# Seven low parts of the second layer's weights: from an adding DMA to a subtraction on VectorE

## The chip, the cores and the metric

The kernel runs on one core of one Trainium2 chip. The metric is the device time of one execution in microseconds (us), the median of several. TensorE is PE in the profile (PEld is its loading of weights), VectorE is DVE, ScalarE is ACT, GpSimd is POOL, SyncE is SP; a "q" behind an engine's name is its queue of DMA instructions.

## The reference, cut to what matters

Two layers over 256 latent tokens and 256 context tokens of 1024 channels. In the second layer (the last) the context gives keys and values only, so nearly all of its products run over 256 columns.

```python
for l in range(DEPTH):
    h = modulate(rmsnorm(x, norm1_g[l]), sh1, sc1)
    p = h @ w_in[l]                      # GLU, q, k, v, branch gates
    y_conv = conv_branch(p[..., :GLU_END], ...)   # depthwise conv of 31 taps, layernorm, silu, w_conv_out
    y_attn = merge_heads(neighbourhood_attention(q, k, v, k_c, v_c, rpb)) @ w_na_out[l]
    x = x + g1 * gated_merge(p[..., QKV_END:], y_conv, y_attn, w_out[l])
    h2 = modulate(rmsnorm(x, norm2_g[l]), sh2, sc2)
    x = x + g2 * conv_ffn(h2, w_up[l], ffn_dw[l], ffn_dw_b[l], w_down[l])
```

All of it is float32.

## The kernel before

Activations lie with their channels on the 128 partitions. The weights come in units of 128 x 1024 float32 (512 KB), each loaded by one DMA of SP into a tile `raw`. TensorE multiplies a narrower form of float32, so every operand is split into a high part and a low part (what the high part leaves), and each product is three matmuls (`mm3`): high weight by high input (L187), high weight by low input (L188), low weight by high input (L189). `group` does this for the eight 128 x 128 blocks of a unit, 24 matmuls into one PSUM bank; PSUM has four banks of the kind `main`.

The high part `whi` of a unit is a cast on ScalarE (L168 or L206). The low part `wlo` is made in one of two ways, and the table `ADDED` of (layer, unit) says which:

```python
    def wadded(l, u):
        r = raw_unit(wall[l, u])
        ...
        act.copy(hi, r)                             # L206
        act.mul(lo, hi.bitcast(F32), -1.0)          # L207
        pool.dma_start(lo, r, accum_op=ALU.add)     # L208
    def unit8(l, u, at=None):
        w = wadded(l, u) if (l, u) in ADDED else wunit(l, u, at)
```

In `wadded` ScalarE writes the negative of the high part and a DMA issued by GpSimd adds `raw` to it in SBUF. In `wunit` VectorE subtracts the high part from `raw` (L169, in `wparts`). `raw`, `whi` and `wlo` have four buffers each, so a unit's cast can begin when the unit four before it is used up.

The order of the work on each engine is set by the tile framework's scheduler, which weighs its own estimates of when each instruction can start; so a different way of making a low part also moves the instructions around it. Each engine then works its list off in order. SP's list of loads is in order too.

The second layer runs in this order: GLU and values; in turn a gate tile, a query tile and a key tile (`gate(ea, 0)`, `qk(1)`, `gate(ea, 1)`, `qk(2)`, `gate(ea, 2)`, `qk(3)`), with the softmax of earlier head pairs (L501 on VectorE, L504 and L507 on ScalarE) and the taps of the depthwise convolution (L659, VectorE) mixed in; the other gate tiles; the layer norm of the convolution's result; the two branch products; their gated sum (`z`, tiles `h`: L982 and L983 on VectorE, L984 on ScalarE, L985 on VectorE); eight units of the output projection (`U_WO`) with the residual (L990); the second norm; 22 pairs of units of the up-projection (`U_UP`: the i-th pair has unit i and unit 22+i, with the convolution of width 3 in L1053 on ScalarE and L1054 and L1057 on VectorE, then L1066, L1069, L1079, L1080); the down-projection.

Of the input projection (`U_IN`), unit 6+j holds the queries of head pair j, unit 10+j its keys, unit 14+n gate tile n.

Of the kernel before, what the change touches and what calls it, by code (L numbers as in the profile page):

```python
# [43 lines left out]

U_GLU0, U_V, U_IN, U_NA, U_CO, U_WO, U_UP, U_DN = 0, 2, 6, 36, 40, 44, 52, 96
NU = 118
ADDED = {*((0, U_IN + i) for i in (*range(19), 20, 22, 24, 26, 28)), *((0, u) for u in (U_NA + 1, U_NA + 3, *range(U_CO, U_CO + 4))), *((1, U_IN + i) for i in (7, 8, 9, 14, 15, 16)), (1, U_WO), *((1, U_UP + i) for i in (4, 5, 6))}
T_GLU, T_Q, T_K, T_GATE = 0, 6, 10, 14

SWAP16 = [(i + 16) % 32 for i in range(32)]  # L50
# [3 lines left out]
def trunk(ctx: ExitStack, tc: tile.TileContext, xt, cvec, crow, wall, wada, params, bias_t, rope_t, out):  # L54
# [123 lines left out]
    def wunit(l, u, at=None, cuts=1):  # L178
        w, more = wparts(l, u, at, cuts)
        more()  # L180
        return w

    def cols(w, i):
        return sl(w[0], i), sl(w[1], i)
# [16 lines left out]
    def wadded(l, u):  # L201

        r = raw_unit(wall[l, u])
        hi = wp.tile([P, UW], F32R, tag="whi", bufs=4, name=nm("whi"))
        lo = wp.tile([P, UW], F32R, tag="wlo", bufs=4, name=nm("wlo"))
# [3 lines that stand above are left out]
        return hi, lo  # L209

    def unit8(l, u, at=None):
        w = wadded(l, u) if (l, u) in ADDED else wunit(l, u, at)
        return [cols(w, i) for i in range(KD)]
# [404 lines left out]
    for l in range(DEPTH):  # L618
# [5 lines left out]
        with ExitStack() if last else start as e1a:  # L624
# [285 lines left out]
            with ExitStack() as e1c:  # L910
# [57 lines left out]
                def branch(base, xh, xl):  # L968
                    for n in range(0, KD, 2):
                        w = (wadded if (l, base + n // 2) in ADDED else wunit)(l, base + n // 2)  # L970
                        for i in range(2):
# [354 lines left out]
```

## Time and profile before

| what | before |
|---|---|
| median of 3 runs | 1116.0 us (1113.12 to 1118.12) |
| profiled execution | 1116.28 us, of which the span from first to last instruction is 1114.5 us |
| mean granted TensorE clock | 0.996 |
| busy share of the span: PE, PEld, DVE, ACT, POOL | 98%, 85%, 80%, 52%, 4% |
| adding transfers (`wlo<-raw`) | 40 of 512 KB, median 5.7 us from issue to landing |
| of these in the second layer | 10, issued from 762.34 to 946.62 us |

The second layer begins near 735 us of the span. A row of the timeline has the start in us, the duration in us, the engine, the line, the operation with output and inputs, and in brackets how long the engine was idle before it and what ended that. The end of a matmul is modelled, so how fast TensorE goes is read from the starts of successive matmuls.

### The profile page before, as it was taken

How to read it: one execution, taken by the hardware profiler on the slowest of the kernel's cores; microseconds unless marked ns; L12 is line 12 of the kernel's file. 1: busy time of each engine (PE TensorE's matmuls, PEld its weight loads, DVE VectorE, ACT ScalarE, POOL GpSimd, SP SyncE). 2: the span in 40 equal slices, each digit the busy share in tenths (PEclk: the TensorE clock that was granted, in tenths of full speed). 3: DMA queues.
4: the chain of work that ended last, by engine and by line, in shares of the span. 5: the costliest groups of instructions: out<-in, count | busy, mean ns of one | idle time of the engine just before them, and what ended most of it. 6: DMA issues, size and time to landing. Idle time of an engine off the chain costs nothing.

```text
span 1114.5 us, 18085 instructions
## 1 busy us (share of the span) xinstructions
PE 1096.1 (98%) x6896; PEld 952.3 (85%) x6896; DVE 887.7 (80%) x1623; ACT 575.9 (52%) x950; POOL 49.2 (4%) x66
## 2 busy tenths in 40 slices
PE   9999999999999999999999999999999999999997
PEld 7777777788889888888888888989799998999997
DVE  5568998889988888888887456797898886888773
ACT  4458766444334543434343223545875667666642
POOL 1011110011000000000000000001000000000000
PEclk9999999999999999999999999999999999999999
DMA  9988674988833454545467566548844584766681
GB/s 369 289 214 228 136 170 108 285 245 220 256 114 114 133 169 142 179 133 165 157 210 237 175 193 210 184 146 234 222 146 150 149 286 136 226 188 186 209 269 57
DMA packets 61238, 212.93 MB, mean 191 GB/s; under 512 B 7392, under 2 KB 7648, under 8 KB 61152
## 3 DMA queue, kind: packets, MB, share of 16 engines
q1 hardware_dynamic: 55104, 190.77, 52.9%
q0 software_dynamic: 5760, 20.97, 9.9%
q8 instruction: 54, 0.88, 0.3%
q14 instruction: 32, 0.26, 0.1%
q10 hardware_dynamic: 288, 0.04, 0.0%
HBM read 187.63 MB, written 1.05 MB: 169 GB/s over the span
## 4 chain that ended last, share of the span: by engine, by line
PE 89%; ACT 3%; DMA 3%; DVE 2%; issue 2%; SPq 1%; POOL 0%; DVEq 0%; ACTq 0%; POOLq 0%
PE main L187 26%; PE main L189 26%; PE main L188 26%; PE main L723 4%; DMA wlo<-raw 2%; SPq L715 1%; PE sc L187 1%; PE sc L188 1%; PE sc L189 1%; PE po L220 1%; PE po L563 1%; DVE cb L659 1%; ACT whi L206 1%; PE sc L137 1%; ACT wlo L207 1%
## 5 line engine op out<-in xcount | busy, mean ns | idle before, releaser
L189 PE MATMUL main<-h,wlo 128*128 128x256 f32 (+1 forms) x1328 | 444.8, 336 | 8.4 <-DMA wlo<-raw 8.4
L187 PE MATMUL main<-h,whi 128*128 128x256 f32 (+1 forms) x1328 | 447.8, 338 | 0.0
L188 PE MATMUL main<-h,whi 128*128 128x256 f32 (+1 forms) x1328 | 443.1, 334 | 0.1
L168 ACT CAST whi<-raw 128x1024 fp32r<-128x1024 f32 (+1 forms) x204 | 211.1, 1038 | 255.8 <-PE main L188 122.3
L169 DVE TENSOR_TENSOR wlo<-raw,whi 128x1024 fp32r<-128x1024 f32 (+1 forms) x204 | 245.2, 1207 | 99.6 <-ACT whi L168 91.9
L189 PEld LDWEIGHTS main<-h,wlo 128*128 128x128 f32 x1328 | 250.4, 189 | 37.8 <-DMA wlo<-raw 9.4
L187 PEld LDWEIGHTS main<-h,whi 128*128 128x128 f32 x1328 | 250.4, 189 | 30.3 <-issue 1.9
L188 PEld LDWEIGHTS main<-h,whi 128*128 128x128 f32 x1328 | 250.6, 189 | 28.5 <-DVE h L390 0.5
L659 DVE SCALAR_TENSOR_TENSOR cb<-u,par,cb 128x512 f32<-128x512 f32 (+1 forms) x240 | 144.6, 620 | 2.8
L188 PE MATMUL main<-fl,whi 128*128 128x256 f32 (+1 forms) x386 | 123.1, 319 | 0.0
L189 PE MATMUL main<-fh,wlo 128*128 128x256 f32 (+1 forms) x386 | 122.9, 318 | 0.0
L187 PE MATMUL main<-fh,whi 128*128 128x256 f32 (+1 forms) x386 | 122.8, 319 | 0.0
L293 DVE CUSTOM_DVE_ANT_0 t<-raw,sb,par 128x1024 bf16<-128x1024 f32 x72 | 91.6, 1280 | 0.8 <-DMA raw<-in_wada 0.5
L188 PEld LDWEIGHTS main<-fl,whi 128*128 128x128 f32 x386 | 72.7, 188 | 5.7 <-DVE fl L1080 0.2
L189 PEld LDWEIGHTS main<-fh,wlo 128*128 128x128 f32 x386 | 72.7, 188 | 5.6
L187 PEld LDWEIGHTS main<-fh,whi 128*128 128x128 f32 x386 | 72.6, 188 | 5.6
L206 ACT CAST whi<-raw 128x1024 fp32r<-128x1024 f32 x40 | 42.1, 1052 | 56.5 <-PE main L188 47.3
L1053 ACT ACTIVATE t<-main,par 128x512 f32<-128x512 f32 (+1 forms) x82 | 51.0, 670 | 36.8 <-PE main L189 36.7
L293 DVE CUSTOM_DVE_ANT_0 t<-own,sb,par 128x1024 bf16<-128x1024 f32 x48 | 60.5, 1282 | 2.0 <-DMA own<-in_wada 2.0
L1054 DVE SCALAR_TENSOR_TENSOR t<-main,par,t 128x510 f32<-128x510 f32 (+1 forms) x82 | 47.3, 615 | 10.8 <-ACT t L1053 10.7
L208 POOL DMA_DIRECT2D wlo<-raw x40 | 35.1, 878 | 314.9 <-ACT wlo L207 185.2
L1057 DVE SCALAR_TENSOR_TENSOR t<-main,par,t 128x510 f32<-128x510 f32 (+1 forms) x82 | 46.9, 612 | 0.0
(215 smaller groups left out, 1267.2 us busy)
## 6 DMA issues: line engine op xcount, KB each, us to landing
raw<-in_wall SPq DMA_DIRECT2D x239, 512.0 KB, 4.3
raw<-in_wada SPq DMA_DIRECT2D x64, 512.0 KB, 4.5
wlo<-raw POOLq DMA_DIRECT2D x40, 512.0 KB, 5.7
own<-in_wada SPq DMA_DIRECT2D x24, 512.0 KB, 5.7
bias<-in_bias_t SPq DMA_DIRECT2D x8, 520.0 KB, 5.5
row<-in_wada SPq DMA_DIRECT2D x8, 512.0 KB, 4.9
sb<-in_crow SPq DMA_DIRECT2D x5, 512.0 KB, 4.9
x<-in_xt SPq DMA_DIRECT2D x8, 256.0 KB, 3.9
```

What stands on the lines that cost most here:

```text
L168: act.copy(hi[:, c], r[:, c])
L169: dve.tensor_tensor(lo[:, c], r[:, c], hi[:, c].bitcast(F32), ALU.subtract)
L187: pe.matmul(ps, w[0], xh, start=start, stop=False)
L188: pe.matmul(ps, w[0], xl, start=False, stop=False)
L189: pe.matmul(ps, w[1], xh, start=False, stop=stop)
L206: act.copy(hi, r)
L293: dve.tensor_tensor_reduce(tmp().bitcast(BF16), r, v, 1.0, pr(l, BADA + n, 1), ALU.mult, ALU.add, mods[l][:, n, s : s + 1])
L659: dve.scalar_tensor_tensor(cb[j], src, w, cb[j], ALU.mult, ALU.add)
L723: mm = pe.matmul(pv[t], h1[n == 1][k][:, c], w[n == 2][:, b], start=k + n == 0, stop=k == KD - 1 and n == 2)
L1053: act.activation(c, pv_, AF.Identity, bias=pr(l, FDB + t, 1), scale=w[1])
L1054: dve.scalar_tensor_tensor(c[:, :, 1:], pv_[:, :, : S - 1], w[0], c[:, :, 1:], ALU.mult, ALU.add)
L1057: dve.scalar_tensor_tensor(c[:, :, : S - 1], pv_[:, :, 1:], w[2], c[:, :, : S - 1], ALU.mult, ALU.add)
```

## The change

Seven entries of `ADDED` for the second layer are taken out; three stay.

```diff
-ADDED = {..., *((1, U_IN + i) for i in (7, 8, 9, 14, 15, 16)), (1, U_WO), *((1, U_UP + i) for i in (4, 5, 6))}
+ADDED = {..., *((1, U_IN + i) for i in (7, 8, 16))}
```

The queries of head pairs 1 and 2 and gate tile 2 keep the adding DMA. Gate tiles 0 and 1, the queries of head pair 3, the first unit of the output projection, and units 4, 5 and 6 of the up-projection get their low part from VectorE. The entries of the first layer (`...` above) are the same. So seven multiplications (L207), seven adding DMAs (L208) go, and seven subtractions (L169) come.

How VectorE's list changes is seen at three places. The numbers behind the names are those of the program as written and differ by a few between the two kernels. First the place of the queries of head pair 3. Before, where `wlo_7671` is the low part of the keys of pair 3, `wlo_7817` that of gate tile 3, and `sc_7523` the scores of pair 1:

```order
L849 TENSOR_TENSOR t_7448<-t_7443,t_7444 128x256
L659 SCALAR_TENSOR_TENSOR cb_2_6581<-u_2_6594,par,cb_2_6581 128x256
L169 TENSOR_TENSOR wlo_7671<-raw_7669,whi_7670 128x1024
L867 SCALAR_TENSOR_TENSOR qk_7450<-t_7448,qk_7450 128x256
L659 SCALAR_TENSOR_TENSOR cb_2_6581<-u_2_6594,par,cb_2_6581 128x256
L844 TENSOR_TENSOR t_7571<-main_7453,rope_6591 128x256
L845 STREAM_SHUFFLE t_7572<-main_7453 128x256
L169 TENSOR_TENSOR wlo_7817<-raw_7815,whi_7816 128x1024
L501 ISA sc_7523,mx_7539<-sc_7523,bias_7224 128x416
```

Now, where `wlo_7623` is the queries of pair 3, `wlo_7668` the keys and `wlo_7814` gate tile 3:

```order
L849 TENSOR_TENSOR t_7446<-t_7441,t_7442 128x256
L659 SCALAR_TENSOR_TENSOR cb_2_6581<-u_2_6594,par,cb_2_6581 128x256
L169 TENSOR_TENSOR wlo_7623<-raw_7621,whi_7622 128x1024
L867 SCALAR_TENSOR_TENSOR qk_7448<-t_7446,qk_7448 128x256
L659 SCALAR_TENSOR_TENSOR cb_2_6581<-u_2_6594,par,cb_2_6581 128x256
L169 TENSOR_TENSOR wlo_7668<-raw_7666,whi_7667 128x1024
L844 TENSOR_TENSOR t_7569<-main_7451,rope_6591 128x256
L845 STREAM_SHUFFLE t_7570<-main_7451 128x256
L169 TENSOR_TENSOR wlo_7814<-raw_7812,whi_7813 128x1024
L501 ISA sc_7521,mx_7537<-sc_7521,bias_7223 128x416
```

The new subtraction takes the slot of the keys' one, and the first softmax instruction of the scores (L501) stands one subtraction later.

The second place is the end of the gated sum `z`, ahead of the output projection. VectorE before, where `wlo_8893`, `wlo_8930` and `wlo_8967` are units 1, 2 and 3 of `U_WO`, and `h_8476` is the low part of the last tile of `z`:

```order
L983 TENSOR_TENSOR t_8805<-t_8805,g_14_8422 128x256
L169 TENSOR_TENSOR wlo_8893<-raw_8891,whi_8892 128x1024
L982 SCALAR_TENSOR_TENSOR t_8823<-g_7_8088,main_8810 128x256
L985 SCALAR_TENSOR_TENSOR h_8475<-t_8805,h_8467 128x256
L983 TENSOR_TENSOR t_8823<-t_8823,g_15_8459 128x256
L169 TENSOR_TENSOR wlo_8930<-raw_8928,whi_8929 128x1024
L985 SCALAR_TENSOR_TENSOR h_8476<-t_8823,h_8468 128x256
L169 TENSOR_TENSOR wlo_8967<-raw_8965,whi_8966 128x1024
```

Now, where `wlo_8854`, `wlo_8889` and `wlo_8926` are units 0, 1 and 2:

```order
L983 TENSOR_TENSOR t_8802<-t_8802,g_14_8419 128x256
L169 TENSOR_TENSOR wlo_8854<-raw_8852,whi_8853 128x1024
L982 SCALAR_TENSOR_TENSOR t_8820<-g_7_8085,main_8807 128x256
L985 SCALAR_TENSOR_TENSOR h_8472<-t_8802,h_8464 128x256
L983 TENSOR_TENSOR t_8820<-t_8820,g_15_8456 128x256
L169 TENSOR_TENSOR wlo_8889<-raw_8887,whi_8888 128x1024
L985 SCALAR_TENSOR_TENSOR h_8473<-t_8820,h_8465 128x256
L169 TENSOR_TENSOR wlo_8926<-raw_8924,whi_8925 128x1024
```

Unit 0 takes the slot that unit 1 had, and units 1 and 2 move back by one slot; as many subtractions as before stand ahead of the last tile of `z`.

The third place is the up-projection. VectorE now, where `wlo_9604` is unit 22+5, `wlo_9674` unit 6, and `main_9543` and `main_9518` the two products of pair 4:

```order
L169 TENSOR_TENSOR wlo_9604<-raw_9602,whi_9603 128x1024
L1080 TENSOR_TENSOR fl_0_9503<-t_9497,fh_0_9502 128x256
L1054 SCALAR_TENSOR_TENSOR t_9568<-main_9543,par,t_9568 128x255
L1054 SCALAR_TENSOR_TENSOR t_9573<-main_9518,par,t_9573 128x255
L1057 SCALAR_TENSOR_TENSOR t_9568<-main_9543,par,t_9568 128x255
L1057 SCALAR_TENSOR_TENSOR t_9573<-main_9518,par,t_9573 128x255
L1054 SCALAR_TENSOR_TENSOR t_9582<-u_3_9337,par,t_9582 128x255
L1054 SCALAR_TENSOR_TENSOR t_9587<-u_2_9332,par,t_9587 128x255
L1069 TENSOR_TENSOR t_9573<-t_9573,t_9568 128x256
L1057 SCALAR_TENSOR_TENSOR t_9582<-u_3_9337,par,t_9582 128x255
L1057 SCALAR_TENSOR_TENSOR t_9587<-u_2_9332,par,t_9587 128x255
L1080 TENSOR_TENSOR fl_4_9579<-t_9573,fh_4_9578 128x256
```

Behind these stand one more L1069 and then the subtraction for unit 6 (`wlo_9674`); before, that low part came by DMA and did not stand on VectorE. Units 4 and 5 (`wlo_9508`, `wlo_9598`) stand ahead of the first and behind the last convolution step of pair 2. TensorE's list is the same up to the output projection. There, and in the up-projection, matmuls that need no low part are drawn ahead of one that does: before at pairs 4 and 5, now at the output projection's first three units (L187 and L188 of each) and at pair 6.

SP's list of loads changes in one point: the load of `sb` (the row of c for the last modulation) stands behind the fifth unit of the output projection now, behind the second load for the up-projection before, and two of the `row` loads move up likewise.

More of the change, by code (lines that the diff above doesn't have):

```diff
@@ L46 @@
 NU = 118
-ADDED = {*((0, U_IN + i) for i in (*range(19), 20, 22, 24, 26, 28)), *((0, u) for u in (U_NA + 1, U_NA + 3, *range(U_CO, U_CO + 4))), *((1, U_IN + i) for i in (7, 8, 9, 14, 15, 16)), (1, U_WO), *((1, U_UP + i) for i in (4, 5, 6))}
+ADDED = {*((0, U_IN + i) for i in (*range(19), 20, 22, 24, 26, 28)), *((0, u) for u in (U_NA + 1, U_NA + 3, *range(U_CO, U_CO + 4))), *((1, U_IN + i) for i in (7, 8, 16))}
 T_GLU, T_Q, T_K, T_GATE = 0, 6, 10, 14
```

## The prediction

> **What bounds the kernel now.** I read the page's first part, then what TensorE waits for, then the starts of its matmuls around those waits.
>
> ```profile
> PE 1096.1 (98%) x6896; PEld 952.3 (85%) x6896; DVE 887.7 (80%) x1623; ACT 575.9 (52%) x950; POOL 49.2 (4%) x66
> ```
>
> TensorE is the bound: 98% busy. A change of low parts can gain only what TensorE loses, and lose whatever it adds to TensorE's waits. The view of waits, for TensorE (in total, times, longest):
>
> ```profile
> PE main L189 <- DMA wlo<-raw: 8.4, 5, 2.5
> ```
>
> Five times it waits for an adding DMA. The timeline of TensorE places them, in the queries of pair 3, unit 0 of the output projection, and units 4, 5 and 6 of the up-projection; all five are units that the change takes off the DMA.
>
> ```profile
> 800.61 0.28 PE L188 MATMUL main<-h,whi 128*128 128x256 f32 x1
> 803.40 0.39 PE L189 MATMUL main<-h,wlo 128*128 128x256 f32 x1 [2.51 <-DMA wlo<-raw]
> 803.63 0.28 PE L187 MATMUL main<-h,whi 128*128 128x256 f32 x1
> 803.75 0.28 PE L188 MATMUL main<-h,whi 128*128 128x256 f32 x1
> ...
> 884.55 0.28 PE L187 MATMUL main<-h,whi 128*128 128x256 f32 x1
> ...
> 885.03 0.28 PE L187 MATMUL main<-h,whi 128*128 128x256 f32 x1
> 887.62 0.38 PE L189 MATMUL main<-h,wlo 128*128 128x256 f32 x1 [2.32 <-DMA wlo<-raw]
> ...
> 934.59 0.28 PE L187 MATMUL main<-h,whi 128*128 128x256 f32 x1
> ...
> 936.05 0.28 PE L187 MATMUL main<-h,whi 128*128 128x256 f32 x1
> 938.18 0.50 PE L189 MATMUL main<-h,wlo 128*128 128x256 f32 x1 [1.85 <-DMA wlo<-raw]
> ...
> 941.67 0.30 PE L187 MATMUL main<-h,whi 128*128 128x256 f32 x1
> ...
> 945.36 0.28 PE L187 MATMUL main<-h,whi 128*128 128x256 f32 x1
> 945.89 0.38 PE L189 MATMUL main<-h,wlo 128*128 128x256 f32 x1 [0.25 <-DMA wlo<-raw]
> ...
> 950.33 0.28 PE L188 MATMUL main<-h,whi 128*128 128x256 f32 x1
> 952.12 0.39 PE L189 MATMUL main<-h,wlo 128*128 128x256 f32 x1 [1.50 <-DMA wlo<-raw]
> ```
>
> A normal step is 0.12 us (803.63 to 803.75); the first step after a wait is 0.23 (803.40 to 803.63). What each wait costs is the step over the normal one plus 0.11 for that restart: queries 2.79 - 0.12 + 0.11 = 2.78; output unit 0 2.59 - 0.12 + 0.11 = 2.58; up-projection unit 5 0.53 - 0.12 + 0.11 = 0.52; unit 6 1.79 - 0.12 + 0.11 = 1.78. At unit 4 the step is 2.13, so 2.01, and then the steps stay long. The windows view (length, busy of PE, PEld, DVE, ACT and POOL, granted clock, DMA share, GB/s) shows why:
>
> ```profile
> 780.00:820.00 40.00, 37.49 (x301) 32.26 (x300) 35.89 (x105) 30.49 (x67) 2.49 (x3) 1.00 0.74 204
> 938.18:940.00 1.82, 1.82 (x9) 1.82 (x10) 1.82 (x6) 1.31 (x3) 0.41 (x1) 0.53 0.75 225
> ```
>
> The granted clock falls to 0.53. From 938.18 to 941.67 there are 16 steps in 3.49 us, where 16 x 0.117 = 1.87 would do: 1.62 more, so unit 4 costs 3.63. Sum of the five places: 2.78 + 2.58 + 3.63 + 0.52 + 1.78 = 11.3 us, the most the change can give back here.
>
> **The change part by part.** What goes: seven multiplications and seven adding DMAs.
>
> ```profile
> 794.62 0.88 POOL L208 DMA_DIRECT2D wlo<-raw  x1 [1.45 <-ACT wlo L207]
> 882.11 0.90 POOL L208 DMA_DIRECT2D wlo<-raw  x1 [13.58 <-PE main L189]
> ...
> DMA to landing us min/median/max: 4.4/5.7/11.8
> ...
> L207 ACT ACTIVATE wlo<-whi x40: 1047/1062/1106, 45.7 to 945.2; 128x1024 fp32r<-128x1024 f32 x40
> ...
> L169 DVE TENSOR_TENSOR wlo<-raw,whi x204: 686/1224/1258, 22.6 to 1095.6; 128x1024 fp32r<-128x1024 f32 x99, 128x512 fp32r<-128x512 f32 x3
> ```
>
> The queries' transfer was issued at 794.62 and TensorE got it at 803.40, 8.8 us; output unit 0 took 882.11 to 887.62, 5.5 us. A subtraction takes 1.22 us, 1.14 from start to start. The 7 x 1.06 = 7.4 us on ScalarE, 52% busy, are counted at nothing either way. VectorE takes 7 x 1.14 = 8.0 us more; its place decides.
>
> *Gate tiles 0 and 1.* Their transfers came in time, so nothing is gained. The timeline of VectorE for this and the next item:
>
> ```profile
> 776.84 0.43 DVE L844 TENSOR_TENSOR t<-main,rope 128x256 f32<-128x256 f32 x1 [3.94 <-PE main L189]
> ...
> 794.83 1.22 DVE L169 TENSOR_TENSOR wlo<-raw,whi 128x1024 fp32r<-128x1024 f32 x1
> ...
> 806.32 0.42 DVE L844 TENSOR_TENSOR t<-main,rope 128x256 f32<-128x256 f32 x1 [0.70 <-PE main L189]
> ...
> 858.96 1.23 DVE L169 TENSOR_TENSOR wlo<-raw,whi 128x1024 fp32r<-128x1024 f32 x1 [1.38 <-ACT whi L168]
> ```
>
> VectorE stands idle 3.94 us ahead of 776.84, so 2.3 us of subtractions are hidden there: 0. If that cover were gone, 2.3.
>
> *Queries of pair 3.* The subtraction takes the slot of 794.83 and ends near 796, TensorE wants it at 800.73: 2.78 gained. Everything behind it on VectorE, the softmax's L501 first, is 1.14 later, and TensorE arrives 2.8 earlier. In 780 to 820 VectorE is busy 35.89 of 40 us; the lag of 3.9 is taken up by its idle times, 0.70 at 806.32, 1.38 at 858.96 and some smaller. I count nothing lost, with one subtraction (1.14) as the other bound.
>
> *Output unit 0.* The subtraction stands where that of unit 1 stood:
>
> ```profile
> 884.68 1.22 DVE L169 TENSOR_TENSOR wlo<-raw,whi 128x1024 fp32r<-128x1024 f32 x1
> ...
> 887.10 1.22 DVE L169 TENSOR_TENSOR wlo<-raw,whi 128x1024 fp32r<-128x1024 f32 x1
> 888.24 0.42 DVE L985 SCALAR_TENSOR_TENSOR h<-t,h 128x256 fp32r<-128x256 f32 x1
> ```
>
> It ends at 885.9. TensorE has six high-part matmuls drawn ahead, 884.55 to 885.25, so it waits 0.65 and restarts for 0.11, in place of 2.58. Unit 1's subtraction ends at 888.32, about when the first unit's other matmuls (some 20 steps from 886) are done, and the last tile of `z` gets its low part at 888.66, some 0.2 late. 1.0 us stays, 1.6 is gained. Bounds: all 2.58, or 0.4 if TensorE waits for one subtraction more.
>
> *Units 4, 5 and 6 of the up-projection.* ScalarE's and then VectorE's timeline:
>
> ```profile
> 928.35 1.05 ACT L206 CAST whi<-raw 128x1024 fp32r<-128x1024 f32 x1 [0.86 <-ACT rstd L1100]
> ```
> ```profile
> 931.50 0.94 DVE L1054 SCALAR_TENSOR_TENSOR t<-main,par,t 128x255 f32<-128x255 f32 x2 [2.42 <-ACT t L1053]
> ...
> 936.83 0.94 DVE L1054 SCALAR_TENSOR_TENSOR t<-main,par,t 128x255 f32<-128x255 f32 x2
> 937.68 0.86 DVE L1057 SCALAR_TENSOR_TENSOR t<-main,par,t 128x255 f32<-128x255 f32 x2
> ...
> 944.23 0.42 DVE L1069 TENSOR_TENSOR t<-t,t 128x256 f32<-128x256 f32 x1
> ```
>
> Unit 4 is cast by 929.40, and VectorE is idle 2.42 us ahead of 931.50: its low part is there near 930.6, wanted at 934.8. The wait and the half clock behind it go: 3.63. Unit 5's subtraction stands behind pair 2's convolution, well ahead of its use: 0.52. Unit 6's stands behind eight convolution steps (0.85 for two, so 0.4 each) and three additions (0.34 each) that need pair 4's products: 4.3 us. Pair 4 starts at 934.59 and ends 48 x 0.117 later, 940.2; with ScalarE's step between, VectorE begins near 941.4 and the subtraction ends near 946.9. TensorE wants it after pair 5 and four matmuls drawn ahead, 934.59 + 100 x 0.117 = 946.3. So it waits some 0.7 and restarts for 0.1: 1.0 of the 1.78 is gained. Bounds: 1.78, or nothing.
>
> Sum: 2.78 + 1.6 + 3.63 + 0.52 + 1.0 = 9.5 us. The profiled execution took 1116.28, 0.3 above the median of the runs, so I forecast **1106.8**. Bounds of the terms: 11.3 (1105.0) and 2.78 - 1.14 + 0.4 + 3.63 + 0.52 = 6.2 (1110.1).
>
> [...] Rows: a step of 2.13 us brought the clock to 0.53, steps of 2.79 and 2.59 did not. [...]
>
> **The rivals.**
>
> *The half clock stays.* It came after the shortest of the three long waits, so it may hang on the moment rather than on the wait, and fall on one of the new waits (0.7 at output unit 0, 0.7 at unit 6). Then 1.62 is not gained: 1108.4. Against it: it is seen nowhere in these rows without a wait.
>
> *VectorE is late everywhere.* If at the queries, the softmax behind them, output unit 0, unit 4 and unit 6 TensorE waits for one subtraction more than I count, that is 5 x 1.14 = 5.7: 1112.5. For it speaks the 35.89 of 40 us in 780 to 820; against it the idle times quoted. [...]
>
> *SyncE's queue, the slower side.* The load of `sb` now stands ahead of the load for output unit 5. The queue is in order, and if `sb`'s tile is not free then, all loads behind it wait. SyncE's timeline, and the custom instruction that reads `sb`, in the stretch from 700 on:
>
> ```profile
> 888.09 0.34 SPq L165 DMA_DIRECT2D raw<-in_wall  x1
> ...
> 896.04 0.38 SPq L271 DMA_DIRECT2D sb<-in_crow  x1
> ```
> ```profile
> L293 DVE CUSTOM_DVE_ANT_0 t<-row,sb,par x8: 1274/1279/1284, 1051.2 to 1082.9; 128x1024 bf16<-128x1024 f32 x8
> ```
>
> The page's part on DMA issues (count, KB, median us to landing):
>
> ```profile
> raw<-in_wall SPq DMA_DIRECT2D x239, 512.0 KB, 4.3
> ```
>
> Unit 5's load went at 888.09. If the tile came free only with the residual of unit 4, near 898, that load would go at 898.4, and load, cast and subtraction (4.3 + 1.05 + 1.22) end at 905.0. TensorE would start on unit 5 at 884.55 + 120 x 0.117 + 1.0 = 899.6, less the 2.8 gained at the queries, 896.8. It would wait 8.2, and 1.6 for the half clock behind it: 1116.6, slower than before; 1120.9 if `sb`, 512 KB too, lands first. I take 1117. It decides from a release at 897.4 on, where the 9.2 to the median are eaten up; later than 898 it can't be, as unit 5 waits behind it. Against it: nothing of this layer reads `sb` before 1051, so the tile's last reader lies before 700.
>
> That the change does not do what it says is excluded by the order of instructions.
>
> **How the numbers follow.** What a measurement of this kernel can tell from no change is about 0.5%, 5.6 us: 1110.4 and 1121.6. Chances: forecast 0.50; half clock stays 0.15; VectorE late 0.20, of which 0.02 under 1110.4; SyncE's queue 0.10; 0.05 for a loss over 5.6 us that no row here shows. Faster 0.50 + 0.15 + 0.02 = 0.67; same 0.18 + 0.10 = 0.28; slower 0.05. The range goes from 1103.5 (the bound 1105.0 less 1.5, part of the spread of the runs, 1113 to 1118) to 1113.5 (VectorE late, and 1 more): it leaves out the queue and the unseen, 0.15.
>
> **What would show it.** Right: no TensorE wait for `wlo` by DMA in the second layer; at the queries, and at units 4 and 5, no wait of any kind; waits of under 1 us at output unit 0 and unit 6, on VectorE; clock 1.00 from 936 to 942. Wrong: a TensorE wait of over 1 us on L169, on the softmax or on `z`; a new stretch at half clock; or SyncE waiting at `sb` while unit 5's cast stands idle.

## The result, and the profile after

The changed kernel took 1107.29 us (median of 5 runs, 1105.99 to 1108.29) against 1116.0: a ratio of 0.9916, with a 95% interval of 0.989 to 0.9943. In a second comparison it took 1106.93 against 1114.99 (0.9923, 0.9903 to 0.9943). The forecast was 1106.8. The total came out; several of its terms did not, and the experiments were needed to see it.

The page's first part, of the changed kernel, whose span is 1106.5 us:

```profile
PE 1094.5 (99%) x6896; PEld 951.2 (86%) x6896; DVE 896.3 (81%) x1630; ACT 567.9 (51%) x943; POOL 42.9 (4%) x59
```

VectorE has 8.6 us more and ScalarE 8.0 less, near the 8.0 and 7.4 counted. What TensorE waits for in the second layer now (from the view of waits: total, times, longest):

```profile
PE main L189 <- DVE wlo L169: 1.1, 2, 0.6
...
PE pt L358 <- DVE ss L344: 0.4, 1, 0.4
```

The row for the adding DMA (8.4 us before) is gone; two short waits for a subtraction stand in its place, and one in the second norm. TensorE's timeline at the queries of pair 3, output unit 0, the second norm, and units 4 and 6 of the up-projection:

```profile
801.19 0.28 PE L188 MATMUL main<-h,whi 128*128 128x256 f32 x1
801.32 0.28 PE L189 MATMUL main<-h,wlo 128*128 128x256 f32 x1
...
883.03 0.28 PE L188 MATMUL main<-h,whi 128*128 128x256 f32 x1
883.84 0.39 PE L189 MATMUL main<-h,wlo 128*128 128x256 f32 x1 [0.52 <-DVE wlo L169]
...
913.73 0.28 PE L189 MATMUL main<-h,wlo 128*128 128x258 f32 x1
914.42 0.38 PE L358 MATMUL pt<-one,ss 128*128 128x1 f32 x2 [0.41 <-DVE ss L344]
...
931.93 0.28 PE L188 MATMUL main<-h,whi 128*128 128x256 f32 x1
932.05 0.28 PE L189 MATMUL main<-h,wlo 128*128 128x256 f32 x1
...
943.53 0.28 PE L188 MATMUL main<-h,whi 128*128 128x256 f32 x1
944.39 0.39 PE L189 MATMUL main<-h,wlo 128*128 128x256 f32 x1 [0.57 <-DVE wlo L169]
```

At the queries and at unit 4 the step to the low part is a normal 0.12. At output unit 0 it is 0.81, 0.69 too long, and at unit 6 0.86, 0.74 too long; the prediction had 0.65 and 0.7. The wait in the second norm was not foreseen. VectorE's rows behind the two, and SyncE's:

```profile
882.56 1.22 DVE L169 TENSOR_TENSOR wlo<-raw,whi 128x1024 fp32r<-128x1024 f32 x1
...
943.11 1.22 DVE L169 TENSOR_TENSOR wlo<-raw,whi 128x1024 fp32r<-128x1024 f32 x1
```
```profile
885.36 0.33 SPq L271 DMA_DIRECT2D sb<-in_crow  x1
886.46 3.32 SPq L165 DMA_DIRECT2D raw<-in_wall  x3
```

Both subtractions run until just before TensorE's step: to 883.78 (882.56 + 1.22) and 944.33 (943.11 + 1.22). The load of `sb` went at 885.36 and the load behind it 1.1 us later, so the queue rival did not come about. The windows view (columns as in the prediction: length, busy of PE, PEld, DVE, ACT and POOL, granted clock, DMA share, GB/s) of 780 to 820, on which the VectorE rival rested, and then of units 4 to 6 of the up-projection, behind the first of which the clock was at half before:

```profile
780.00:820.00 40.00, 40.00 (x321) 34.83 (x320) 36.20 (x105) 28.91 (x64) 1.59 (x2) 1.00 0.58 164
931.82:945.00 13.18, 12.61 (x107) 12.40 (x106) 13.18 (x31) 12.03 (x24) 0.00 (x0) 1.00 0.41 121
```

The clock is 1.00 in both. TensorE works through 780 to 820 without a pause, while VectorE is busy 36.20 of the 40 us; from 931.82 to 945 VectorE has no pause at all, and TensorE has only the wait at unit 6.

### The profile page after: what moved, and what is told of

Read it like the earlier page. It is cut to its first block, busy times and chain, and to the rows that moved or that the text cites. A ratio compares the mean times of both kernels' runs of the same rounds, so it can differ in the third digit from the quotient of the medians.

```text
span 1106.5 us, 18047 instructions
## 1 busy us (share of the span) xinstructions
PE 1094.5 (99%) x6896; PEld 951.2 (86%) x6896; DVE 896.3 (81%) x1630; ACT 567.9 (51%) x943; POOL 42.9 (4%) x59
## 4 chain that ended last, share of the span: by engine, by line
PE 87%; DVE 4%; ACT 3%; DMA 3%; SPq 1%; issue 1%; DVEq 0%; ACTq 0%
PE main L187 25%; PE main L189 25%; PE main L188 25%; PE main L723 4%; DMA raw<-in_wall 2%; SPq L715 1%; PE sc L187 1%; PE sc L188 1%; PE sc L189 1%; DVE wlo L169 1%; PE po L220 1%; PE po L563 1%; ACT whi L168 1%; DVE cb L659 1%; PE sc L480 1%
## 5 line engine op out<-in xcount | busy, mean ns | idle before, releaser
L187 PE MATMUL main<-h,whi 128*128 128x256 f32 (+1 forms) x1328 | 447.3, 337 | 0.0
L188 PE MATMUL main<-h,whi 128*128 128x256 f32 (+1 forms) x1328 | 442.5, 334 | 0.1
L168 ACT CAST whi<-raw 128x1024 fp32r<-128x1024 f32 (+1 forms) x211 | 217.7, 1036 | 243.2 <-DMA raw<-in_wall 120.3
L169 DVE TENSOR_TENSOR wlo<-raw,whi 128x1024 fp32r<-128x1024 f32 (+1 forms) x211 | 253.1, 1207 | 90.8 <-ACT whi L168 87.7
L187 PEld LDWEIGHTS main<-h,whi 128*128 128x128 f32 x1328 | 249.5, 188 | 30.4 <-issue 2.2
L188 PEld LDWEIGHTS main<-h,whi 128*128 128x128 f32 x1328 | 249.8, 188 | 28.5 <-DVE h L390 0.5
L187 PE MATMUL main<-fh,whi 128*128 128x256 f32 (+1 forms) x386 | 123.0, 319 | 0.0
L188 PE MATMUL main<-fl,whi 128*128 128x256 f32 (+1 forms) x386 | 122.9, 318 | 0.0
L188 PEld LDWEIGHTS main<-fl,whi 128*128 128x128 f32 x386 | 72.7, 188 | 5.6
L187 PEld LDWEIGHTS main<-fh,whi 128*128 128x128 f32 x386 | 72.7, 188 | 5.5
L206 ACT CAST whi<-raw 128x1024 fp32r<-128x1024 f32 x33 | 34.6, 1050 | 49.8 <-PE main L188 42.3
L389 ACT ACTIVATE h<-t,mod 128x256 fp32r<-128x256 f32 x56 | 25.1, 501 | 34.8 <-DVE t L388 34.7
```

The lines of the kernel that those rows point to most:

```text
L168: act.copy(hi[:, c], r[:, c])
L169: dve.tensor_tensor(lo[:, c], r[:, c], hi[:, c].bitcast(F32), ALU.subtract)
L187: pe.matmul(ps, w[0], xh, start=start, stop=False)
L188: pe.matmul(ps, w[0], xl, start=False, stop=False)
```

## The experiments

What ran: parts of the change alone, two parts of it undone one at a time, the transfers that were left removed as well, two attempts at the new waits, the changed kernel again and the kernel before twice again. All edits but two are of the table `ADDED`.

**Parts alone.** The first takes only gate tiles 0 and 1 off the DMA:

```diff
-... (1, U_IN + i) for i in (7, 8, 9, 14, 15, 16)
+... (1, U_IN + i) for i in (7, 8, 9, 16)
```

> Against the kernel before, only gate tiles 0 and 1 of the second layer are taken from the adding DMA. Theory (VectorE's idle time ahead of 776 hides two subtractions): the five waits of TensorE for the DMA stay, 11.3 us in all, and the time is that before, within 0.5 us in the profile. Rival (VectorE is late by a subtraction wherever one is added): 1.1 to 2.3 us slower, seen as TensorE waits near 784 to 800.

Measured: 1114.36 us against 1115.13 (0.9981, 0.9963 to 0.9998). The second takes only the queries of pair 3 off it (`(7, 8, 14, 15, 16)`):

> Against the kernel before, only the queries of pair 3 are taken from the adding DMA. Theory: the wait of 2.78 us there goes and nothing takes its place, 2.8 us faster (ratio 0.9975). Rival (the softmax behind the new subtraction is late by it): a new wait of up to 1.14 us between 803 and 825, 1.6 us faster. The waits at output unit 0 and at units 4 to 6 of the up-projection stay, or grow by what VectorE and the loads do not follow; if the half clock hangs on the length of the wait at unit 4 it stays, if it hangs on the moment it may go or turn up at another wait, since everything behind the queries comes 2.8 us earlier.

Measured: 1114.14 against 1115.13 (0.998, 0.9962 to 0.9998). The third takes only `(1, U_WO)` out:

> Against the kernel before, only unit 0 of the output projection is taken from the adding DMA. The scheduler again puts the load of sb among the output projection's loads and the first row load two weight loads earlier. Theory: 2.58 us of wait become 1.1, 1.4 us faster. For the wait of 0.7 us that the changed kernel shows new in the second norm there are two readings. If the early row load is its cause, it shows here too, 0.4 to 0.8 us, and the gain is 0.6 to 1.0. If the cause is that TensorE comes 3.5 us earlier there, it does not show, since TensorE comes only 1.4 us earlier.

Measured: 1113.01 against 1115.13 (0.9976, 0.9956 to 0.9996). The fourth takes only units 4, 5 and 6 of the up-projection out:

> Against the kernel before, only units 4, 5 and 6 of the up-projection are taken from the adding DMA; TensorE is not earlier ahead of them. Theory: the waits and the half clock there, 5.9 us, become one wait of 0.7 and a restart, 5.1 us faster (ratio 0.9954), more than half of what the whole change gained. Rival (the half clock hangs on the moment): 1.6 us less, with half clock at another wait. The waits at the queries and at output unit 0 stay at 2.78 and 2.58.

Measured: 1109.18 against 1115.13 (0.9941, 0.9921 to 0.9962). TensorE's waits for the DMA in these four, one row of the view of waits each (gates, q3, wo, up):

```profile
PE main L189 <- DMA wlo<-raw: 6.5, 3, 2.6
```
```profile
PE main L189 <- DMA wlo<-raw: 6.6, 3, 2.9
```
```profile
PE main L189 <- DMA wlo<-raw: 4.2, 2, 2.5
```
```profile
PE main L189 <- DMA wlo<-raw: 2.2, 1, 2.2
```

The up-projection carries most of the change, 6.0 us by medians where 5.1 was expected; `wo` has 2.1 where 1.4 was expected, and `q3` 1.0 where 2.8 was. Each interval is about 2 us to either side, so differences of a microsecond between the parts are not measured. But the counts surprise. In gates, wo and up the queries of pair 3 are still on the DMA, and none of the three waits there: of the five places of before, gates should have kept five and has three (output unit 0, units 4 and 5). So the queries' wait of 2.5 us is not a cost that this transfer has every time. q3 has no wait to remove, its ratio is that of gates, and its output unit 0 waits longer (2.9) than before (2.32).

**Was the profile of before typical?** The kernel before was profiled twice more.

> The kernel before, a second profile. If the wait at the queries of pair 3 is a fixed cost: 2.5 us again. If it was one late transfer: none, while output unit 0 and units 4 and 5 of the up-projection wait 2.4, 1.9 and 0.4 to 2.7 us as in all other profiles that keep them on the DMA. The half clock at 938 comes again if it follows the wait at unit 4, and not if it hangs on the moment.

> The kernel before, a third profile, for the same question: how often TensorE waits at the queries of pair 3, and how often a wait of 2 us is followed by a stretch at half clock. By the granted clock of the timed runs of before, 0.991 to 0.998, from none to four such stretches of 3.5 us fall in one execution.

Measured: 1114.45 and 1114.65 us. The waits for the DMA, before_again and then before_third:

```profile
PE main L189 <- DMA wlo<-raw: 5.7, 3, 2.3
```
```profile
PE main L189 <- DMA wlo<-raw: 6.6, 4, 2.3
```

Neither waits at the queries. The timeline of before_again there, and its first wait:

```profile
799.95 0.28 PE L188 MATMUL main<-h,whi 128*128 128x256 f32 x1
800.07 0.28 PE L189 MATMUL main<-h,wlo 128*128 128x256 f32 x1
...
884.93 0.39 PE L189 MATMUL main<-h,wlo 128*128 128x256 f32 x1 [2.33 <-DMA wlo<-raw]
```

Its transfer was issued at 794.63, as in the first profile (794.62); there it was there for TensorE at 803.40, here in time for 800.07. The windows view for the stretches behind the waits (columns as before: length, PE, PEld, DVE, ACT, POOL, clock, DMA share, GB/s), of before_again:

```profile
886.50:889.70 3.20, 3.20 (x17) 3.20 (x16) 0.74 (x1) 0.00 (x0) 0.00 (x0) 0.50 0.98 365
...
937.60:940.80 3.20, 3.20 (x17) 3.20 (x16) 2.58 (x5) 0.48 (x2) 0.87 (x1) 0.50 0.90 233
```

of before_third:

```profile
886.00:889.20 3.20, 3.20 (x17) 3.20 (x16) 1.83 (x3) 0.00 (x0) 0.00 (x0) 0.50 0.78 269
937.50:940.70 3.20, 3.20 (x28) 3.20 (x29) 3.20 (x7) 1.75 (x3) 0.87 (x1) 1.00 0.81 251
```

and of gates and of q3:

```profile
946.50:949.70 3.20, 3.20 (x17) 3.20 (x17) 1.57 (x4) 1.04 (x1) 0.00 (x0) 0.50 0.80 210
```
```profile
886.20:889.40 3.20, 3.20 (x27) 3.20 (x28) 2.29 (x3) 0.14 (x1) 0.00 (x0) 1.00 0.67 207
936.50:939.70 3.20, 3.20 (x28) 3.20 (x29) 3.20 (x7) 1.85 (x4) 0.89 (x1) 1.00 0.91 270
944.40:947.60 3.20, 3.20 (x28) 3.20 (x29) 3.08 (x7) 2.18 (x5) 0.00 (x0) 1.00 1.01 165
```

The half clock moves: in the first profile behind unit 4, in the second behind output unit 0 and unit 4, in the third behind output unit 0 only, in gates behind unit 5, in q3 nowhere. Where it falls, 17 matmuls pass in 3.2 us in place of 27 or 28. Over the eight profiles with adding transfers that TensorE waits for (the three of before, gates, q3, wo, up and awo below) there are 18 steps of 2.0 to 3.2 us in this layer, and 5 of them are followed by a stretch at half clock: 0.12 us after the step in the first profile (938.18 to 938.30), and by the rows above not later than 1.63 us after it in gates (944.87 to 946.50). In the first profile of the changed kernel, one of the six without such a step, the clock is 1.00 in every stretch of 1 us from 0 to 1099; the other five have a mean clock of 0.997 or 0.998. The granted clock of the timed runs is from 0.991 to 0.998 in the 35 of the kernel before that ran beside these four parts, 0.997 or 0.998 in all 11 of the changed kernel.

**Where the half clock fell.** In the first profile of before the clock is 0.50 from 938.30 to 941.71, 3.41 us, and falls again at 1108.96, at the end of the program, where TensorE runs out of work. In the first profile of the changed kernel it falls only there, at 1099.76. The windows view over stretches as long as that half clock: three of before with a long wait in them and the one behind the third, then one of before_third, then two of q3. In before and before_third the author laid them back from the start of a half clock in whole lengths, in q3 from the fall at the end:

```profile
801.77:805.18 3.41, 1.77 (x15) 1.78 (x16) 3.34 (x11) 3.41 (x10) 0.00 (x0) 1.00 0.54 137
883.69:887.10 3.41, 1.62 (x14) 1.41 (x12) 3.21 (x8) 1.42 (x3) 0.00 (x0) 1.00 0.96 227
934.89:938.30 3.41, 1.56 (x12) 1.26 (x12) 2.41 (x7) 3.41 (x8) 0.00 (x0) 1.00 0.98 202
938.30:941.71 3.41, 3.41 (x17) 3.41 (x18) 3.29 (x7) 1.19 (x2) 0.87 (x1) 0.50 0.79 258
```
```profile
882.47:885.88 3.41, 1.14 (x10) 0.93 (x9) 3.10 (x6) 1.78 (x3) 0.00 (x0) 1.00 0.71 141
```
```profile
881.20:884.61 3.41, 2.07 (x18) 1.86 (x16) 2.94 (x7) 1.37 (x3) 0.00 (x0) 1.00 1.00 253
884.61:888.03 3.42, 1.87 (x15) 1.88 (x16) 2.90 (x5) 0.90 (x3) 0.00 (x0) 1.00 0.33 59
```

Two of these windows have a half clock behind them: the third of before, in which TensorE is busy for 1.56 us, and the one of before_third, with 1.14. Behind the other four with a wait in them, busy for 1.77, 1.62, 2.07 and 1.87 us, the clock stays at 1.00. The step of 3.17 us in q3 falls into two of the windows, and no half clock follows; the step of 2.13 at unit 4 of before lies in one, and one follows. So the length of the step alone does not tell them apart. That the busy time of one such window does is the author's estimate from these six; no run changed that alone.

**The queries once more.** The changed kernel, with `(1, U_IN + 9)` back in the table:

> The changed kernel with the queries of pair 3 on the adding DMA again. If the wait of 2.5 us that the profile of before showed there is a fixed cost of that transfer: 2.8 us slower than the changed kernel, 1110.1. If it was one late transfer, as its absence in the runs gates, wo and up says: TensorE waits nothing there and the time is that of the changed kernel, 1107.3, with some runs 2 to 4 us above the others.

The changed kernel itself ran beside it:

> The changed kernel once more, as the base of the other three: 1107.3 us, clock 0.997 to 0.998 in nearly every run, waits of 0.7 at output unit 0, 0.6 to 0.8 in the second norm and 0.7 at unit 6 of the up-projection.

Measured: 1106.80 us for aq3 and 1106.93 for the changed kernel (ratios 0.9925, 0.9902 to 0.9947, and 0.9923, 0.9903 to 0.9943); TensorE waits nothing at the queries in aq3. That part of the change is worth nothing that can be measured.

**Output unit 0 undone.** The changed kernel with `(1, U_WO)` back in the table:

> The changed kernel with unit 0 of the output projection on the adding DMA again. Theory: a wait of 2.4 to 2.6 us in place of 1.1 in all, 1.3 us slower than the changed kernel, 1108.3, with some runs 2 us higher and a lower clock where the wait brings a stretch at half rate. Rival (what the subtraction saves there is lost again behind it, at the second norm): the time of the changed kernel, 1107.

Measured: 1108.19 us (0.9932, 0.9913 to 0.9951). Its waits for a low part:

```profile
PE main L189 <- DMA wlo<-raw: 2.4, 1, 2.4
...
PE main L189 <- DVE wlo L169: 0.6, 1, 0.6
```

By medians against 1106.93 it is 1.3 slower, as the theory had it, but against the next kernel, `none`, which ran beside it, it is 0.5 slower. The intervals overlap in both cases, so the size rests on the waits, 2.4 against 0.5.

**No transfers at all.** The changed kernel with `*()` for the last three entries of this layer:

> The changed kernel without the three adding transfers that are left in the second layer (queries of pairs 1 and 2, gate tile 2), so that VectorE makes every low part there. Theory (VectorE has idle time near 770 to 783, and TensorE uses these units 6 us or more after their cast): no new wait of TensorE, the time of the changed kernel, 1107, within 0.5 us. Rival (the next subtractions are those that saturate VectorE, so a few transfers must stay): waits of 1.1 us or more at the softmax between 784 and 830, 1108 to 1110.

Measured: 1107.67 us (0.9923, 0.9903 to 0.9944), the ratio of the changed kernel. TensorE's waits for low parts have the same row as in the changed kernel (1.1 in all, 2 times, 0.6 the longest), so three more subtractions cost nothing. The windows view shows what they fill, of the changed kernel and then of none:

```profile
770.00:785.00 15.00, 15.00 (x105) 13.36 (x104) 9.47 (x22) 7.52 (x11) 0.87 (x1) 1.00 0.87 238
785.00:800.00 15.00, 15.00 (x119) 13.03 (x119) 13.77 (x38) 12.04 (x26) 1.59 (x2) 1.00 0.56 150
```
```profile
770.00:785.00 15.00, 15.00 (x105) 13.36 (x105) 11.77 (x23) 6.82 (x12) 0.00 (x0) 1.00 0.52 169
785.00:800.00 15.00, 15.00 (x120) 13.03 (x119) 15.00 (x44) 12.06 (x26) 0.74 (x1) 1.00 0.38 109
```

Even with VectorE busy through all of 785 to 800, TensorE goes on without a pause there.

**The new waits.** In the changed kernel's first profile the second norm waits because ScalarE does:

```profile
912.54 1.06 ACT L168 CAST whi<-raw 128x1024 fp32r<-128x1024 f32 x1 [1.68 <-DMA raw<-in_wall]
913.50 0.41 ACT L340 ACTIVATE t<-x 128x256 f32<-128x256 f32 x1
```

The last square (L340) stands behind a cast whose weight comes late. One suspect was the load of a `row`, which now stands two loads earlier. a_row holds the row loads behind a weight load of the up-projection:

```diff
-                units.append(raw_unit(wada[l, n], place()))
+                with tc.issue_after(mark[0].ins) if mark else ExitStack(): units.append(...)
...
-                ffn_out(i, pa, pg)
+                mark.extend([lastdma[0]] if last and i == 9 else []); ffn_out(i, pa, pg)
```

> The changed kernel with the loads of the first two rows of the last modulation held behind a weight load in the middle of the up-projection. If the early row load is what makes a weight land late ahead of the second norm: the waits of 0.26 and 0.58 us near 908 and 914 go, 0.8 us faster than the changed kernel, 1106.5. If it is TensorE's earlier arrival, they stay, and the time is 1107.3.

Measured: 1106.54 us (0.992, 0.99 to 0.994), and no wait in the norm. But the second profile of the unchanged changed kernel has none there either, so this does not show that the row load is the cause. wo has the wait, 0.4 us, with the early row load, and gates has 0.2 without it. It is left open; the wait comes in some executions and not in others of the same kernel. a_best also halves two units:

```diff
-    w = wadded(l, u) if (l, u) in ADDED else wunit(l, u, at)
+    w = wadded(l, u) if (l, u) in ADDED else wunit(l, u, at, 2 if (l, u) in HALVES else 1)
     # HALVES = {(1, U_WO), (1, U_UP + 6)}
```

> The changed kernel with the row loads held back as in a_row, and unit 0 of the output projection and unit 6 of the up-projection loaded, cast and subtracted in two halves, so that TensorE can start on the first half. Theory: the waits of 0.7 us at those two places shrink to 0.1 to 0.2 each, and with the norm's that is 1.8 us faster than the changed kernel, 1105.5. Rival (the halves cost more on VectorE and ScalarE than they save, two instructions for one): no gain, 1107.3, with the waits a few steps later.

Measured: 1106.37 us (0.9918, 0.9898 to 0.9938), the lowest median of all, yet not to be told from the changed kernel's 1106.93. The long waits went, but not to zero, and at the up-projection one shows a unit later:

```profile
945.15 0.39 PE L189 MATMUL main<-h,wlo 128*128 128x256 f32 x1 [0.29 <-DVE wlo L169]
```

This step, 0.57 us long, belongs to unit 22+6, right behind unit 6, whose own step to the low part is now 0.38. Together they are 0.71 over the normal steps, where unit 6 alone was 0.74 over: VectorE is late by about the same amount, and the wait moves on to the next unit.

## Why the prediction was right, and where it was right for the wrong reason

- *The five waits go, and short ones take their place at output unit 0 and unit 6.* Right, with sizes: 0.69 for 0.65, 0.74 for 0.7. The reading of the order, which subtraction stands in whose slot and what must be done ahead of it, held to 0.1 us. The wait in the second norm of the first profile was not in the forecast.
- *Gate tiles cost nothing.* Right for TensorE, whose waits gates does not lengthen at this place; the ratio's interval, 0.9963 to 0.9998, is even a little below 1, and which executions make it so is not shown.
- *Queries of pair 3, 2.78 us.* Wrong: the step that failed is taking a wait from one profile as the cost of the transfer. Seven profiles here have this unit on the DMA, and one waits. The signs were in the rows: issued 794.62, wanted 800.73, so 6.1 us, against a median landing of 5.7. A transfer that is in time on the median is a chance, not a cost.
- *Output unit 0, 1.6 us.* Right, as far as it can be measured: 2.1 by the medians of wo and 1.3 or 0.5 by those of awo. By the steps it is 2.47 + 0.11 less 0.69 + 0.11, so 1.8, less some 0.3 for the last tile of `z`, whose low part comes late as foreseen (three steps of 0.26, 0.22 and 0.21 from 886.44 to 887.00 in the changed kernel).
- *Unit 4, with 1.62 us for the half clock.* The wait went. The half clock is a term of the wrong kind: it does not belong to unit 4. The three profiles of before have 8 steps of 2.0 us or more and 4 stretches at half clock, two behind unit 4 and two behind output unit 0, so one stretch in the sum was near the truth while its place was luck. The rival that the half clock stays was right that it hangs on the moment, but not on that alone: in the first profile of the changed kernel, where no wait of this layer's products is over 0.57 us, the clock is 1.00 up to 1099.
- *Units 5 and 6, 0.52 and 1.78 us before.* Mis-sized one by one, since the half clock at unit 4 in the first profile, 1.62 us, made TensorE that much later at unit 5, where it waited 0.25. Without one, unit 5 waits 1.8 (before_third) to 2.6 (gates).
- *VectorE late at five places, 1112.5.* It did not come about: none shows no cost at the queries and the softmax, with VectorE busy 15.00 of 15 us, and aq3, with the queries' subtraction taken away again, is no faster.
- *SyncE's queue, 1117.* It did not come about: in the changed kernel, behind unit 0, TensorE has no wait for a unit of the output projection over 0.3 us.

So where did the 8 to 9 us come from? Steps over the normal one plus 0.11 of restart each, in the two later profiles of before: 2.49 + 2.03 + 1.68 + 0.33, and two half clocks of 1.6, are 9.7; 2.43 + 1.99 + 1.96 + 0.84 + 0.44, and one half clock, are 9.3. The changed kernel keeps 0.69 + 0.74 + 0.22, 1.65, and the 0.3 at the last tile of `z`. That leaves 7.8 and 7.3 us; the spans of these two profiles, 1112.7 and 1112.9, are 7.8 and 8.0 above the 1104.9 of after_again. The two comparisons of medians gave 8.7 and 8.1. Without the 2.78 of the late query the forecast's own terms add up to 6.75. So the one late transfer stood in for what the first profile happened to lack, a second half clock or a long wait at unit 5, and that the total came within 0.5 us of the measured time is in part luck.

Not explained: 8 of those 35 runs of the kernel before took 1119.3 to 1122.3 us, with granted clocks of 0.994 down to 0.991. No profile caught one, so how many of the other microseconds are late transfers and how many half clocks stays open.

## What to carry to other kernels

A wait in one profile is a sample: set the time between a transfer's issue and its use beside the spread of its landings (6.1 us beside 4.4 to 11.8 here), and charge the wait in full only where the use comes before the fastest landing. The order of instructions gave the waits on engines to a tenth of a microsecond here; what hung on DMA landings and on the clock varied from execution to execution (the queries' transfer was late in one profile of seven, and the three of before have one, two and one half clocks) and is to be charged as a chance times a price. A long wait cost more than its length here where a half clock followed it: 5 of 18 steps of 2.0 to 3.2 us, at a price of 1.62 us in the first profile. And a busy engine (36 of 40 us here) can take more work if its consumers have slack; look at the slack of who waits, not at the busy share.

## What the runs showed of the hardware

In the first profile of before the granted clock of TensorE was 0.50 from 938.30 to 941.71, 3.41 us, in which 17 matmuls passed, and 1.00 on both sides. In before_again (886.50 and 937.60), before_third (886.00) and gates (946.50) it was 0.50 through 3.2 us with 17 matmuls, where stretches of that length at 1.00 have 27 or 28. These are 5 stretches behind 18 steps of 2.0 to 3.2 us: a step of 2.13 was followed by one, a step of 3.17 was not. Of the six windows of 3.41 us above that have a long wait in them, the two followed by a half clock have TensorE busy for 1.56 and 1.14 us, the other four for 1.62 to 2.07; what sets it is not shown. In the first profile of the changed kernel the waits in this layer's products are 0.57 us and less, and the clock is 1.00 up to 1099; it fell at 1099.76, at the end of the program, in the second of two waits, of 0.70 and 0.61, with 4 matmuls of one column between them.
